# Squares of the gate norm summed in four groups of 32 tokens, one norm pass over 192 columns, and two state scalings placed earlier

## The chip, the cores and the metric

The kernel runs on one core of one Trainium2 chip. The metric is the device time of one execution in microseconds (us): the median of the runs of a kernel, lower is better. The core's engines are TensorE (PE in the profile, its weight loads PEld), VectorE (DVE), ScalarE (ACT), GpSimd (POOL) and SyncE (SP); each works through its own queue of instructions in order, and they wait for one another by semaphores.

## The reference

One layer of a streaming encoder is computed for 512 prompt frames and 64 frames of a running stream (576 tokens in all): a Mamba-2 state-space branch (SSD) and a latent-attention branch (MLA) side by side, an output projection, and a SwiGLU network. The change is about the norm behind the gate of the SSD branch, and about the scaling of the last SSD state:

```python
xbc, conv_new = causal_conv(xbc, conv_buf, p['conv_w'], p['conv_b'])
...
y, h_new = ssd_scan(xh, dt, A, Bm, Cm, ssm_h0)
y = y + d_skip[:, None] * xh
y = y.reshape(b, T, SSD_WIDTH) * jax.nn.silu(z)        # SSD_WIDTH = 512
y_ssd = rmsnorm(y, p['ssd_norm'])                       # per token, over 512 values
...
o_lat = mla_attend(q_lat, q_rope, q_pos, keys_c, keys_r, jnp.arange(P + T))
o = jnp.einsum('bthl,lhd->bthd', o_lat, p['w_uv']).reshape(b, T, MLA_WIDTH)
x = x + jnp.concatenate([y_ssd, o], axis=-1) @ p['w_out']
hf = rmsnorm(x, p['norm_ffn'])
x = x + (jax.nn.silu(hf @ p['w_gate']) * (hf @ p['w_up'])) @ p['w_down']

# ssd_scan, per chunk: w_end is exp(last - cum) * d
h_new = jnp.exp(last)[..., None, None] * h + jnp.einsum('blgh,blghp,blgn->bghpn', w_end, x, Bk)
```

All of it is float32.

## The kernel before

Features lie on partitions and tokens on columns: `xsd` holds the SSD branch's y as four tiles of 128 features x 576 tokens. The tokens come in five chunks: c = 0 to 3 are the prompt, 128 tokens each, and c = 4 is the stream, 64 tokens. Products that need more than one pass over the hi parts of the operands are written as hi x hi, hi x lo and lo x hi (`wh_`, `wl_` tiles, split on ACT by line 127 and on DVE by line 128). A matmul of plain float32 operands stands in the trace as two records.

The stages that the change touches follow one another. In the SSD stage (about 110 to 146 us) the last chunks' scores and states run on PE between the value products `ps_v` and the projections `ps_q`, `ps_k` of the first two attention head pairs. `gate(c)` (lines 624 to 635) multiplies y by the gate on DVE, squares it on ACT into `ysq`, sums the squares of the 512 features by four matmuls with a 128x128 matrix of ones (`ps_g`, line 634), which puts the sum of each token into all 128 partitions, and copies it on ACT into `ssy` (its rows in the trace name the tile R, since `ssy` is that buffer). `norm_y` (lines 806 to 811) turns `ssy` into the factor 1/sqrt(mean + eps), `Ry`, in two halves of 288 tokens. Each half is a chain through two engines: ACT lines 186, 188, 189, and DVE lines 187, 192, 193. `cat_tile(t)` scales a tile of y by `Ry` on DVE (line 814) and splits it in hi and lo parts (`cat_y`).

In the attention stage (146 to 222 us) PE makes scores `sc` of a head pair (line 719), ACT and DVE make the softmax `pr` of them (lines 702 to 709), PE transposes it (`ptp`, line 741), and the output projection `ps_o` (line 465) starts with the SSD half `cat_y`. The stream's scores are `sc_s`, its softmax `pr_4`, its transposes `ptp_s` (line 749). `qs` and `ks` are the copies of the projections `ps_q` and `ps_k` (lines 669, 673).

In the last stage (from 600 us) PE adds the last part of the down projection, `ps_l` (line 1143), DVE adds each finished bank to the stream x (line 1186) so that the bank is free for the next product, and the inputs of the last state products are scaled on DVE: `late_x` by line 500 (`to_chunk_end`) and line 503 (`decay`), called from `late_operands`; the products that read them run on PE after 625 us.

The order of the instructions on each engine is written out: the table ISSUE lists for PE, DVE, ACT, POOL and SP the numbers of the instructions in the order in which they are to be issued, and the table PLACES the buffer or PSUM bank that each tile takes. So the order is that of the tables, not that of the code.

Of the kernel before, what the change touches and what calls it, by code (L numbers as in the profile page):

```python
# [56 lines left out]
def hybrid_layer_kernel(ctx: ExitStack, tc: tile.TileContext, a, o):  # L57
# [206 lines left out]
    ssy = R1  # L264
# [1083 lines left out]
0651423651426340315406516235041350264531645302406124531260546312045123450612345014652051342603541350124365310462054260  # L1348
534132025104623562453163052412365401546210503421602541356041536510223405632140562056143241564032
# [15 lines left out]
0202102121201021020122100210121012012102101202012012012012012021021021021021021021021021021021021021021021021022101201  # L1365
202101
# [18 lines left out]
986 996-998 994-995 1042-1050 1031-1038 1023-1024 1055-1056 1051 1071-1088 1052-1054 1089-1100 1117-1119 1061-1063
1120 1057-1058 1067-1068 1059-1060 1126-1128 1064-1066 1121-1125 1069 1129-1152 1101-1104 1070 1225-1233 1115-1116
1234 1237 1235-1236 1238-1248 1153 1107-1110 1105-1106 1249-1260 1154 1172 1261-1272 1111-1114 1155-1157 1173-1175
1158-1171 1273-1281 1285-1286 1176-1179 1184-1185 1180-1183 1201-1202 1186-1188 1223 1189-1194 1287-1293 1195-1197
1224 1198-1200 1282-1284 1211-1216 1203-1210 1217 1314 1218-1220 1294 1221-1222 1295-1302 1315 1303 1316 1304-1313
1317-1318 1326-1328 1319 1338-1339 1344-1347 1340-1341 1348-1350 1342 1351 1343 1329 1320-1325 1330-1337 1352-1359  # L1390
1364 1360-1362 1365-1366 1363 1367-1389 1400 1390-1392 1401-1402 1393-1399 1403-1411 1424 1412-1423 1425-1429
1436-1437 1430-1431 1438 1432-1435 1568 1439-1443 1448 1444 1449-1452 1445 1453-1454 1446 1455-1456 1447 1457-1458
1583 1574 1580 1459 1577 1569 1460-1474 1575 1475-1482 1571 1484 1483 1485 1581 1486-1493 1496 1494 1497-1499 1495
1582 1584 1500-1502 1572 1570 1503 1576 1504-1505 1508 1573 1509 1506 1510-1511 1507 1512-1513 1601 1514-1518 1589
1519-1521 1578-1579 1522-1523 1602 1524-1527 1598 1532 1528 1533 1529 1534 1530 1599 1535 1603 1531 1585 1536-1537
1595 1538-1540 1590 1604 1541-1546 1596 1547-1548 1591 1610 1549-1551 1605 1556 1552-1553 1622 1557-1561 1611
1554-1555 1562-1564 1612 1565-1566 1600 1567 1592 1586 1593-1594 1597 1587 1606 1613 1616 1619 1617 1631 1623 1618
1588 1632 1625 1633 1624 1607 1637 1614 1626 1620 1627 1608-1609 1621 1654-1655 1638 1640 1646 1656 1643 1657-1658
1628-1629 1659 1647 1644 1660-1661 1615 1652 1634-1636 1662 1639 1663 1630 1664 1641 1665 1642 1645 1648-1650 1653
1690 1666-1668 1691-1693 1669 1678 1694 1651 1670 1695 1671 1696 1714 1679 1715 1672-1673 1697 1674 1680 1698 1675  # L1400
1681 1699 1676 1700 1682 1677 1716 1683 1717 1684 1718-1719 1685 1720 1686-1687 1702 1688-1689 1721 1703 1722 1701
# [274 lines left out]
```

## Time and profile before

| | before |
|---|---|
| time, median of 3 runs | 635.87 us (635.25 to 636.33) |
| profiled execution: its time / its span | 637.53 us / 635.6 us |
| TensorE granted clock over the span | 0.997 of full speed |
| PE busy | 624.6 us (98%) |
| PEld busy (beside PE) | 595.9 us (94%) |
| DVE busy | 551.9 us (87%) |
| ACT busy | 390.3 us (61%) |
| POOL busy | 70.5 us (11%) |

The span is the stretch from the first to the last instruction in the trace; 1.93 us (637.53 less 635.6) of the profiled execution's time lie around it. An engine's busy time is the sum over its instructions without overlaps, so that what is left of the span is its idle time. A row of the timeline gives the start of a run of like instructions, its length to the end of the last one, engine, line, what is written and read, the shape and the number; in square brackets stands how long the engine was idle before it and on whom it waited. Ends of matmuls are modelled, and a matmul's length holds its passage through the array, so the time that a run of matmuls costs is read from its start to the start of the next row.

### The profile page before, as it was taken

The page shows a single profiled execution, that of the slowest core. Times are in us where ns is not written, and L with a number is a line of the kernel's source. Part 1 is how long each engine was busy: PE and PEld are TensorE (multiplying, and loading weights), DVE is VectorE, ACT ScalarE, POOL GpSimd, SP SyncE. Part 2 cuts the span into 40 slices and gives each one's busy share as a digit, 9 for nine tenths or more (in the row PEclk, how much of TensorE's full clock was granted, in tenths as well). Part 3 has the DMA queues.
Part 4 walks back from the last instruction along what each step waited for, and adds up shares of the span by engine and source line. Part 5 has one row for each costly group of instructions (what it writes and reads, how often), then busy time and mean ns, then how long its engine had stood idle before and what let it go on. Part 6 is the DMA issues. An engine that isn't in the chain of part 4 may idle for free.

```text
span 635.6 us, 11925 instructions
## 1 busy us (share of the span) xinstructions
PE 624.6 (98%) x4613; PEld 595.9 (94%) x4613; DVE 551.9 (87%) x982; ACT 390.3 (61%) x751; POOL 70.5 (11%) x111
## 2 busy tenths in 40 slices
PE   9999999999999999999999999999999999999995
PEld 9899999885797899999999999999999999999994
DVE  6999995789767599999998997889888998999775
ACT  7655425789766479955656555656564666635464
POOL 1322122001010000000012002100111011100023
PEclk9999999999999999999999999999999999999998
DMA  9522175223220232232177436551756154734105
GB/s 317 201 51 79 35 209 163 99 72 130 104 80 35 66 125 76 88 112 68 34 197 166 120 100 150 141 139 52 188 138 157 68 165 117 168 100 160 45 1 182
DMA packets 32888, 74.63 MB, mean 117 GB/s; under 512 B 3882, under 2 KB 11960, under 8 KB 32576
## 3 DMA queue, kind: packets, MB, share of 16 engines
q1 hardware_dynamic: 26688, 62.73, 30.0%
q0 software_dynamic: 5424, 10.57, 9.3%
q8 instruction: 36, 0.59, 0.4%
q10 hardware_dynamic: 720, 0.57, 0.3%
q14 instruction: 20, 0.16, 0.1%
HBM read 59.14 MB, written 4.15 MB: 100 GB/s over the span
## 4 chain that ended last, share of the span: by engine, by line
PE 50%; DVE 1%; ACT 0%; DVEq 0%; issue 0%
PE ps_x L933 17%; PE ps_dx L1073 9%; PE ps_z L933 9%; PE ps_dz L1073 5%; PE ps_y L933 4%; PE ps_l L1143 4%; PE ps_dy L1073 2%; PE ps_s L507 0%; DVE x L1186 0%; PE ps_n L1249 0%; DVE x L1199 0%; DVE x L1203 0%; PE ps_n L1275 0%; DVE late_x L503 0%; DVE late_x L500 0%; PE ps_r L1317 0%
## 5 line engine op out<-in xcount | busy, mean ns | idle before, releaser
L933 PE MATMUL ps_x<-xop,wh_gu_S 128*128 128x288 f32 x504 | 126.3, 295 | 0.0
L933 PEld LDWEIGHTS ps_x<-xop,wh_gu_S 128*128 128x128 f32 x504 | 88.2, 188 | 0.7 <-ACT u L1002 0.2
L933 PE MATMUL ps_x<-xop,wl_gu_S 128*128 128x288 f32 x252 | 73.3, 295 | 0.0
L933 PE MATMUL ps_z<-xop,gu_a 128*128 128x288 f32 x252 | 61.7, 295 | 0.0
L127 ACT CAST wh_gu_S<-gu 128x1024 fp32r<-128x1024 f32 x44 | 46.2, 1053 | 14.8 <-PE ps_y L933 4.2
L128 DVE TENSOR_TENSOR wl_gu_S<-gu,wh_gu_S 128x1024 fp32r<-128x1024 f32 x44 | 52.9, 1219 | 0.8 <-ACT wh_gu_S L127 0.5
L933 PEld LDWEIGHTS ps_x<-xop,wl_gu_S 128*128 128x128 f32 x252 | 47.1, 188 | 0.0
L1086 POOL DMA_DIRECT2D x<-db x16 | 14.8, 927 | 279.6 <-ACT db L1079 249.5
L143 PE MATMUL ps_in<-xs,wh_in 128*128 128x288 f32 x256 | 45.5, 298 | 0.0
L933 PE MATMUL ps_y<-xop,wh_gu_A 128*128 128x288 f32 x168 | 44.9, 296 | 0.0
L933 PEld LDWEIGHTS ps_z<-xop,gu_a 128*128 128x128 f32 x252 | 43.5, 188 | 0.0
L933 PE MATMUL ps_z<-xop,wh_gu_S 128*128 128x288 f32 x168 | 43.4, 295 | 0.0
L933 PE MATMUL ps_x<-xop,wh_gu_A 128*128 128x288 f32 x168 | 42.7, 294 | 0.0
L127 ACT CAST wh_gu_A<-gu 128x1024 fp32r<-128x1024 f32 x22 | 23.1, 1051 | 24.6 <-PE ps_x L933 16.1
L143 PEld LDWEIGHTS ps_in<-xs,wh_in 128*128 128x128 f32 x256 | 37.7, 189 | 0.2
L933 PEld LDWEIGHTS ps_y<-xop,wh_gu_A 128*128 128x128 f32 x168 | 30.1, 188 | 0.1
L933 PEld LDWEIGHTS ps_z<-xop,wh_gu_S 128*128 128x128 f32 x168 | 29.7, 188 | 0.0
L128 DVE TENSOR_TENSOR wl_gu_A<-gu,wh_gu_A 128x1024 fp32r<-128x1024 f32 x22 | 26.8, 1219 | 3.3 <-ACT wh_gu_A L127 1.8
L465 PE MATMUL ps_o<-cat_y,wh_out 128*128 128x288 f32 x128 | 29.1, 313 | 0.5 <-DVE x L797 0.5
L933 PEld LDWEIGHTS ps_x<-xop,wh_gu_A 128*128 128x128 f32 x168 | 29.5, 188 | 0.0
L465 PE MATMUL ps_o<-cat_o,wh_out 128*128 128x288 f32 x128 | 27.5, 298 | 0.0
L143 PE MATMUL ps_in<-xs,wl_in 128*128 128x288 f32 x128 | 27.5, 296 | 0.0
(604 smaller groups left out, 1994.7 us busy)
## 6 DMA issues: line engine op xcount, KB each, us to landing
gu<-in_w_gu SPq DMA_DIRECT2D x44, 512.0 KB, 4.8
db<-in_w_down SPq DMA_DIRECT2D x16, 512.0 KB, 4.2
x<-db POOLq DMA_DIRECT2D x16, 288.0 KB, 6.4
x<-dc POOLq DMA_DIRECT2D x16, 288.0 KB, 4.3
wr_in<-in_w_in SPq DMA_DIRECT2D x8, 512.0 KB, 5.6
wr_out<-in_w_out SPq DMA_DIRECT2D x8, 512.0 KB, 3.2
cumb<-cumD SPq DMA_DIRECT2D x5, 512.0 KB, 4.8
x<-in_xT SPq DMA_DIRECT2D x2, 1152.0 KB, 6.5
```

What stands on the lines that cost most here:

```text
L127: act.copy(hi, raw)
L128: dve.tensor_tensor(lo, raw, hi.bitcast(F32), ALU.subtract)
L143: pe.matmul(ps[:m, hf, :n], w, x[:, hf * n : (hf + 1) * n], start=start and k == 0 and i == 0, stop=stop and k == last and i == 2,)
L465: pe.matmul(ps[:, :n], w, x[:, cols], start=not onto and k == 0 and i == 0, stop=onto or (k == len(terms) - 1 and i == 2), skip_group_chec ...
L933: pe.matmul(ps, p, q, start=not onto and first and kp == kps[0] and j == 0, stop=onto or (last and kp == kps[-1] and j == 2), skip_group_c ...
L1073: pe.matmul(ps, l, r, start=not onto and k == 0 and j == 0, stop=onto or (k == n - 1 and j == 2), skip_group_check=onto,)
L1086: pool.dma_start(x2[t], v, accum_op=ALU.add)
L1143: pe.matmul(ps, w, x[:, cols], start=first and not onto and k == 0 and i == 0, stop=onto or (last and k == len(terms) - 1 and i == 2), ski ...
```

## The change

Three things are changed.

First, in `gate` the squares of a prompt chunk (c < 4) are summed in four groups of 32 tokens: each of the four feature tiles takes four matmuls with 32 columns of ones as weights, and group j of the tokens lands on the PSUM partitions 32j to 32j+31 and on the same 32 columns. `ps_g` is 128x32 then, and chunk c's sums take 32 columns of `ssy`; the stream's 64 columns stand behind the prompt's 128. The stream's chunk (c = 4) is summed as before.

Second, `norm_y` makes the factor in one pass over these 192 columns, in place. The stream's 64 columns are copied on POOL; the prompt's factors, of which each group of 32 partitions holds other tokens, are spread over all partitions by four matmuls, whose weights are one column of the identity repeated 128 times (`ps_ry`), and copied on ACT into `Ry`.

Third, the tables: the two scalings of `late_x` for chunk 3 stand earlier on DVE, the split `wl_pair` of the third pair's weights too, and around the norm the rows are set anew. PE's and SP's order elsewhere is unchanged.

```diff
@@ gate(c) @@
         q = tmp(f"ysq{c}", 4 * L).rearrange("p (t l) -> p t l", t=4)
         act.activation(q, yv, AF.Square)
-        ps = bank("pp", f"ps_g{c}")[:, :L]
+        n = L // 4 if c < 4 else L
+        ps = bank("pp", f"ps_g{c}")[:, :n]
         for t in range(4):
-            pe.matmul(ps, ones, q[:, t], start=t == 0, stop=t == 3)
-        act.copy(ssy[:, tk], ps)
+            if c == 4:
+                pe.matmul(ps, ones, q[:, t], start=t == 0, stop=t == 3)
+                continue
+            for j in range(4):
+                pe.matmul(ps[32 * j : 32 * j + 32], ones[:, :32], q[:, t, j * n : j * n + n], start=t == 0, stop=t == 3)
+        act.copy(ssy[:, n * c : n * c + n] if c < 4 else ssy[:, P : P + n], ps)
@@ norm_y() @@
-        for hf in range(2):
-            cols = slice(hf * TH, (hf + 1) * TH)
-            norm_half(Ry[:, cols], ssy[:, cols], 512)
+        R = ssy[:, : P + TS]
+        norm_half(R, R, 512)
+        pool.tensor_copy(Ry[:, TP:], R[:, P:])
+        ps = bank("pp", "ps_ry")
+        for j in range(4):
+            pe.matmul(
+                ps.rearrange("p (c j n) -> p j c n", c=4, j=4)[:, j], ident[:, 32 * j : 32 * j + 1].to_broadcast([P, P]),
+                R[:, :P].rearrange("p (c n) -> p c n", c=4), start=True, stop=True,
+            )
+        act.copy(Ry[:, :TP], ps)
@@ ISSUE, PE (first changed line of many) @@
-793-816 765-768 817-824 857-859 831-834 860-862 825-830 863-864 835-837 865 878-881 838 866-868 839 843-850 869-871
+793-816 765-768 817-824 869-871 831-834 872-874 825-830 875-876 835-837 877 890-893 838 878-880 855-862 881-883
```

On PE, from the second score product of head pair 0 to the first transposes, these rows stood in this order before (`sc_3_1` is the second head's scores of the fourth query block, `ps_q_1` pair 1's second query projection):

```order
L719 MATMUL sc_3_1_1938<-ks_383,qs_382 128x512
L634 MATMUL ps_g_1873<-ysq_1871,ones 128x128
L719 MATMUL sc_1_0_1962<-ks_383,qs_382 128x256
L634 MATMUL ps_g_1882<-ysq_1880,ones 128x128 x4
L719 MATMUL sc_1_1_1964<-ks_383,qs_382 128x256
L719 MATMUL sc_2_0_1976<-ks_383,qs_382 128x384
L719 MATMUL sc_2_1_1978<-ks_383,qs_382 128x384
L634 MATMUL ps_g_1873<-ysq_1871,ones 128x128 x3
...
L465 MATMUL ps_q_1_1909<-cqn_487,wl_pair_1827 128x288
L725 MATMUL sc_s<-ks_383,qs_382 64x320 x2
L719 MATMUL sc_3_0_2014<-ks_385,qs_384 128x512
L741 MATMUL ptp_0_0_2033<-ident,pr_0_1996 128x128
```

And these stand there now:

```order
L724 MATMUL sc_3_1_1984<-ks_383,qs_382 128x512
L639 MATMUL ps_g_1897<-ysq_1895,ones 32x32 x16
L724 MATMUL sc_1_0_2008<-ks_383,qs_382 128x256
L639 MATMUL ps_g_1918<-ysq_1916,ones 32x32 x16
L724 MATMUL sc_1_1_2010<-ks_383,qs_382 128x256
L724 MATMUL sc_2_0_2022<-ks_383,qs_382 128x384
L724 MATMUL sc_2_1_2024<-ks_383,qs_382 128x384
...
L465 MATMUL ps_q_1_1957<-cqn_487,wl_pair_1851 128x288
L819 MATMUL ps_ry<-R_99,ident 128x4x32 x4
L730 MATMUL sc_s<-ks_383,qs_382 64x320 x2
L724 MATMUL sc_3_0_2060<-ks_385,qs_384 128x512
L746 MATMUL ptp_0_0_2079<-ident,pr_0_2042 128x128
```

The 32-token sums of a chunk stand in one block of 16 ahead of `sc_1_0` and of `sc_1_1`; nothing of them is left behind `sc_2_1`; the four `ps_ry` stand ahead of `sc_s`. The other two chunks' sums, of which before one matmul stood ahead of `ps_y` of chunk 1, two ahead of `ps_q_0`, two ahead of `ps_k_0` and three ahead of `ps_k_1`, are now one block of 16 ahead of `ps_k_0` and one ahead of `ps_k_1`.

On DVE, in the softmax of pair 0 with the norm chain (lines 187, 192 and 193) between its rows, these rows stood before, from the first norm half's last step on:

```order
L193 SCALAR_TENSOR_TENSOR Ry<-nr_u,nr_y 128x288
L187 TENSOR_SCALAR nr_v<-R_99 128x288
L709 TENSOR_SCALAR pr_2_1982<-pr_2_1982,sm 128x384
L702 TENSOR_REDUCE mx<-sc_s 128x1
L669 COPY qs_384<-ps_q_1_1909 64x288
L192 TENSOR_TENSOR nr_u<-nr_u,nr_v 128x288
L704 RECIPROCAL sm<-sm 128x2
L193 SCALAR_TENSOR_TENSOR Ry<-nr_u,nr_y 128x288
L709 TENSOR_SCALAR pr_0_1996<-pr_0_1996,sm 128x128
L702 TENSOR_REDUCE mx<-sc_3_0_2014 128x1
L704 RECIPROCAL sm<-sm 128x1
L814 SCALAR_TENSOR_TENSOR xsd<-xsd,par,Ry 128x576 x2
```

And these stand there now, from the one pass's last two steps on:

```order
L192 TENSOR_TENSOR nr_u<-nr_u,nr_v 128x192
L193 SCALAR_TENSOR_TENSOR R_99<-nr_u,nr_y 128x192
L707 TENSOR_REDUCE mx<-sc_0_1_2038 128x1
L709 RECIPROCAL sm<-sm 128x2
L714 TENSOR_SCALAR pr_2_2028<-pr_2_2028,sm 128x384
L674 COPY qs_384<-ps_q_1_1957 64x288
L709 RECIPROCAL sm<-sm 128x2
L714 TENSOR_SCALAR pr_0_2042<-pr_0_2042,sm 128x128
L707 TENSOR_REDUCE mx<-sc_s 128x1
L826 SCALAR_TENSOR_TENSOR xsd<-xsd,par,Ry 128x576 x2
L707 TENSOR_REDUCE mx<-sc_3_0_2060 128x1
```

The scaling of `pr_0`, for which PE's first transposes wait, no longer stands behind a second norm half and the reduction of `sc_s`.

On DVE near the end, with the sums of the down projection into x, these rows stood before (`ps_l_0` to `ps_l_3` belong to the first half of x, `ps_l_4` to the second):

```order
L500 TENSOR_TENSOR late_x_7349<-late_x_7349,hcw 64x512
L1186 TENSOR_TENSOR x_0_2045<-ps_l_0_7361,x_0_2045 128x320
L1186 TENSOR_TENSOR x_0_2045<-ps_l_1_7362,x_0_2045 128x320
L500 TENSOR_TENSOR late_x_7354<-late_x_7354,hcw 128x512
L503 TENSOR_TENSOR late_x_7354<-late_x_7354,hcw 128x512
L1186 TENSOR_TENSOR x_0_2045<-ps_l_2_7363,x_0_2045 128x320
L1186 TENSOR_TENSOR x_0_2045<-ps_l_3_7364,x_0_2045 128x320
L1186 TENSOR_TENSOR x_1_2047<-ps_l_4_7431,x_1_2047 128x320
```

And these stand there now:

```order
L500 TENSOR_TENSOR late_x_7395<-late_x_7395,hcw 64x512
L1198 TENSOR_TENSOR x_0_2091<-ps_l_0_7407,x_0_2091 128x320
L500 TENSOR_TENSOR late_x_7400<-late_x_7400,hcw 128x512
L503 TENSOR_TENSOR late_x_7400<-late_x_7400,hcw 128x512
L1198 TENSOR_TENSOR x_0_2091<-ps_l_3_7410,x_0_2091 128x320
L1198 TENSOR_TENSOR x_0_2091<-ps_l_1_7408,x_0_2091 128x320
L1198 TENSOR_TENSOR x_0_2091<-ps_l_2_7409,x_0_2091 128x320
L1198 TENSOR_TENSOR x_1_2093<-ps_l_4_7477,x_1_2093 128x320
```

The two scalings stand one sum earlier, and the sums of `ps_l_1` to `ps_l_3` are in another order.

## Rows read from the trace of the kernel before

**Rows 1.** The page's busy times: us, share of the span, number of instructions.

```profile
PE 624.6 (98%) x4613; PEld 595.9 (94%) x4613; DVE 551.9 (87%) x982; ACT 390.3 (61%) x751; POOL 70.5 (11%) x111
```

**Rows 2.** PE's waits: who for whom, us in total, times, longest.

```profile
PE ptp L741 <- DVE pr L709: 0.9, 1, 0.9
...
PE ps_l L1143 <- DVE x L1186: 0.2, 1, 0.2
PE ptp_s L749 <- DVE pr L709: 0.2, 1, 0.2
```

**Rows 3.** The tile ps_g: instructions, ns min/median/max, first and last start.

```profile
L634 PE MATMUL ps_g<-ysq,ones x40: 217/275/362, 122.6 to 149.9; 128*128 128x128 f32 x32, 128*128 128x64 f32 x8
```

**Rows 4.** Timeline of PE at the sums of squares and scores.

```profile
126.86 0.38 PE L634 MATMUL ps_g<-ysq,ones 128*128 128x128 f32 x2
127.17 1.09 PE L573 MATMUL ps_y<-E,xdt 128*64 128x128 f32 x16
128.20 0.45 PE L652 MATMUL ps_v<-wh_uv,ckv 128*64 128x512 f32 x1
...
146.71 1.05 PE L634 MATMUL ps_g<-ysq,ones 128*128 128x128 f32 x8
147.60 1.90 PE L719 MATMUL sc<-ks,qs 100*128 100x256 f32 x6
```

**Rows 5.** Timeline of PE at products with 64 columns of weights.

```profile
199.70 0.71 PE L777 MATMUL pvs<-pts,V 64*64 64x64 f32 x12
200.34 0.40 PE L465 MATMUL ps_o<-cat_y,wh_out 128*128 128x288 f32 x1
```

**Rows 6.** The same at 199.69 to 199.72 us: records under way.

```profile
199.70 0.27 PE L777 MATMUL pvs<-pts,V 64*64 64x64 f32 x2
```

**Rows 7.** Timeline of ACT and of DVE, first half of the norm.

```profile
148.42 0.53 ACT L186 ACTIVATE nr_y<-R,epsb 128x288 f32<-128x288 f32 x1
...
151.48 0.44 DVE L193 SCALAR_TENSOR_TENSOR Ry<-nr_u,nr_y 128x288 f32<-128x288 f32 x1
```

**Rows 8.** Timeline of DVE, second half of the norm and the scaling behind it.

```profile
153.78 0.46 DVE L193 SCALAR_TENSOR_TENSOR Ry<-nr_u,nr_y 128x288 f32<-128x288 f32 x1
154.16 0.28 DVE L709 TENSOR_SCALAR pr<-pr,sm 128x128 f32<-128x128 f32 x1
```

**Rows 9.** Timeline of PE from sc_s to the first output products.

```profile
151.57 0.76 PE L725 MATMUL sc_s<-ks,qs 100*64 100x320 f32 x4
152.45 1.13 PE L719 MATMUL sc<-ks,qs 100*128 100x512 f32 x2
154.50 0.66 PE L741 MATMUL ptp<-ident,pr 128*128 128x128 f32 x4 [0.92 <-DVE pr L709]
...
157.63 0.41 PE L749 MATMUL ptp_s<-ident,pr 128*64 128x128 f32 x2 [0.22 <-DVE pr L709]
```

**Rows 10.** Timeline of DVE around the split wl_pair.

```profile
141.91 0.46 DVE L669 COPY qs<-ps_q 64x288 f32<-64x288 f32 x1 [0.41 <-ACT qs L669]
...
147.76 0.55 DVE L128 TENSOR_TENSOR wl_pair<-wr_pair,wh_pair 128x384 fp32r<-128x384 f32 x1
```

**Rows 11.** Timeline of DVE in the last stage.

```profile
608.74 0.49 DVE L1186 TENSOR_TENSOR x<-ps_l,x 128x320 f32<-128x320 f32 x1 [1.83 <-PE ps_l L1143]
609.14 0.68 DVE L500 TENSOR_TENSOR late_x<-late_x,hcw 128x512 f32<-128x512 f32 x1
609.74 0.69 DVE L503 TENSOR_TENSOR late_x<-late_x,hcw 128x512 f32<-128x512 f32 x1
610.34 1.68 DVE L1186 TENSOR_TENSOR x<-ps_l,x 128x320 f32<-128x320 f32 x4
```

**Rows 12.** Timeline of PE in the last stage.

```profile
610.71 0.60 PE L1143 MATMUL ps_l<-pr,wh_dl 128*128 128x320 f32 x3
611.15 0.31 PE L1143 MATMUL ps_l<-pr,wl_dl 128*128 128x320 f32 x1
611.68 0.39 PE L1143 MATMUL ps_l<-pr,wh_dl 128*128 128x256 f32 x1 [0.22 <-DVE x L1186]
```

More of the change, by code (lines that the diff above doesn't have):

```diff
@@ L1385 @@
[L1385 to L1389, printed above, removed]
@@ new lines @@
+863-866 884-889 926-928 867-868 894-897 929-931 839-854 932-934 914-925 898-913 935-937 947-956 938-943 957 944-946
+958-960 993-1001 1012-1013 961-976 1014 977-992 1015-1019 1002-1011 1020-1022 1024-1027 1023 1035-1036 1028 1032-1033
+1051 1039-1041 1029-1031 1034 1063 1052-1054 1037 1042-1043 1064-1069 1044 1055-1062 1070-1074 1077-1082 1045
+1091-1093 1038 1048-1050 1046-1047 1094-1102 1083-1090 1075-1076 1107-1108 1103 1123-1140 1104-1106 1141-1152
+1169-1171 1113-1115 1172 1109-1110 1119-1120 1111-1112 1178-1180 1116-1118 1173-1177 1121 1181-1204 1153-1156 1122
@@ new lines @@
+1277-1285 1167-1168 1286 1289 1287-1288 1290-1300 1205 1159-1162 1157-1158 1301-1312 1206 1224 1313-1324 1163-1166
+1207-1209 1225-1227 1210-1223 1325-1333 1337-1338 1228-1231 1236-1237 1232-1235 1253-1254 1238-1240 1275 1241-1246
+1339-1345 1247-1249 1276 1250-1252 1334-1336 1263-1268 1255-1262 1269 1366 1270-1272 1346 1273-1274 1347-1354 1367
+1355 1368 1356-1365 1369-1370 1378-1380 1371 1390-1391 1396-1399 1392-1393 1400-1402 1394 1403 1395 1381 1372-1377
+1382-1389 1404-1411 1416 1412-1414 1417-1418 1415 1419-1441 1452 1442-1444 1453-1454 1445-1451 1455-1463 1476
@@ new lines @@
+1464-1475 1477-1481 1488-1489 1482-1483 1490 1484-1487 1620 1491-1495 1500 1496 1501-1504 1497 1505-1506 1498
+1507-1508 1499 1509-1510 1635 1626 1632 1511 1629 1621 1512-1526 1627 1527-1534 1623 1536 1535 1537 1633 1538-1545
+1548 1546 1549-1551 1547 1634 1636 1552-1554 1624 1622 1555 1628 1556-1557 1560 1625 1561 1558 1562-1563 1559
+1564-1565 1653 1566-1570 1641 1571-1573 1630-1631 1574-1575 1654 1576-1579 1650 1584 1580 1585 1581 1586 1582 1651
+1587 1655 1583 1637 1588-1589 1647 1590-1592 1642 1656 1593-1598 1648 1599-1600 1643 1662 1601-1603 1657 1608
@@ new lines @@
+1604-1605 1674 1609-1613 1663 1606-1607 1614-1616 1664 1617-1618 1652 1619 1644 1638 1645-1646 1649 1639 1658 1665
+1668 1671 1669 1683 1675 1670 1640 1684 1677 1685 1676 1659 1689 1666 1678 1672 1679 1660-1661 1673 1706-1707 1690
+1692 1698 1708 1695 1709-1710 1680-1681 1711 1699 1696 1712-1713 1667 1704 1686-1688 1714 1691 1715 1682 1716 1693
+1717 1694 1697 1700-1702 1705 1742 1718-1720 1743-1745 1721 1730 1746 1703 1722 1747 1723 1748 1766 1731 1767
+1724-1725 1749 1726 1732 1750 1727 1733 1751 1728 1752 1734 1729 1768 1735 1769 1736 1770-1771 1737 1772 1738-1739
@@ new lines @@
+2908-2909 2919 2890-2892 2910 2896-2898 2911 2879-2880 2899 2893 2900 2912-2913 2901-2902 2914 2881 2903 2915
+2904-2905 2920 2916 2921-2923 2917 2942-2943 2924 2930-2935 2944-2945 2936 2954 2925 2955 2926 2946-2947 2937 2948
+2927 2938 2928-2929 2956 2949-2951 2939 2952 2940 2953 2957 2941 2958-2963 2978 2964-2969 2990 2970-2971 2979
+2972-2975 2980 2976-2977 2981 3002 2982 2991 2983 3003 2992 3004 2984 2993-2995 2985 2996 3005 2997 2986 2998 3006
+3080 2999-3001 3007 3081 3008 2987 3082 2988 3009 3026-3028 2989 3029 3010-3011 3083 3030 3012 3031-3032 3084
@@ L1505 @@
+4342 4325 4343 4326 4344 4327 4371 4359 4328-4329 4348-4349 4345 4330-4331 4358 4350 4383-4384 4351 4372 4352-4353
+4332 4354 4360 4333 4355 4361 4373-4374 4385 4356 4375-4376 4395 4357 4386 4396 4387-4388 4362-4363 4389 4364 4397
+4365-4366 4377-4378 4367 4379 4398 4368 4399 4380 4369 4390 4400 4391 4401 4370 4392 4381 4393 4382 4394 4402 4407
+4403-4406 4408-4430
 """,
@@ new lines @@
+829 843 852 842 836-837 844 840 838 854 839 831 830 841 845 847 855 832 856 874 849 859 851 848 850 857-858 861 864
+878 870 860 865 871 875 867 873 866 876 869 872 883 879 884 890 882 900 868 877 881 896 902 880 903 891-892 897 904
+893 885 894 912 899 908 901 905 886 907 906 862 898 913-914 916 863 915 910 887 911 917-918 909 888 921 895 920 930
+919 922 889 931 925 924 932 923 926-927 933 928-929 934 937 935-936 940 938-939 942-943 941 945 944 947 946 948-949
+951 956 952 950 954-955 953 958 960-961 964-965 957 959 962 966 963 967-978
@@ L1565 @@
+684 686 688 690 681 687 685 693 695-697 691 683 698-699 679 700 707 689 694 701 703 705-706 702 708-712 692 704
+713-714 717 716 715
 """,
     "POOL": """
[L1567 to L1568 removed]
+0-3 7 18 28 4 8 5 9 6 10 26-27 11 29 12-17 20-22 19 23-25 31 30 32-42 53 55 57 59 54 56 58 60 43-52 61-74 76 75 77-78
+80 79 81-86 88 87 89-90 92 91 93-94 96 95 97-107 109-110 108 112 111
```

312 lines of the change are left out of this document (140 added, 172 removed).

## The prediction

> **What bounds the kernel now.** I read the busy times first: PE is busy for 624.6 us of the 635.6 us span, 98%, while DVE has 87% and ACT 61% [rows 1]. So PE's instruction stream is the time, and an edit counts by what it takes out of that stream or by what it makes the stream wait. The list of PE's waits comes next. It is short: the first transposes `ptp` wait 0.9 us for DVE's scaling of a softmax, the stream's `ptp_s` 0.2 us for the like, and one down product `ps_l` 0.2 us for DVE's sum into x [rows 2]. All three lie where the change acts. Then the timeline of PE at those places, to see what a matmul costs from its start to the start of the next row, and DVE's and ACT's beside it, to see who is late.
>
> **What is removed on PE.** `ps_g` has 40 records, 32 of them for the prompt (128x128) and 8 for the stream, which stay [rows 3]. Eight of them run from 146.71 us to the start of the next product at 147.60: 0.89 us, 111 ns each [rows 4]. 32 x 0.111 = 3.55 us go.
>
> **What is added on PE: four blocks of 16 small matmuls.** A matmul has two records, so a block has 32, 128 in all. No row of before has a product with 32 columns of weights and 32 of tokens. The nearest are those with 64 columns of weights, of which two run side by side. `ps_y` does 16 records of 128 columns in 1.03 us (127.17 to 128.20) [rows 4]; one after another at 111 ns they would take 1.78 us, in pairs 0.89 us, so they run in pairs and 0.14 us goes for entering and leaving. The two records ahead of it take 0.31 us (126.86 to 127.17) in place of 0.22, so 0.09 us more goes for the change from full weights to half ones. `pvs`, 12 records of 64 columns, takes 0.64 us (199.70 to 200.34) [rows 5]: six pairs at half of 111 ns are 0.33 us, and 0.31 us is for its two shapes. Two records are under way within 0.03 us of its start [rows 6]. If four groups run side by side as two do, and the time of a pass goes with its columns (111 ns x 32/128 = 28 ns), a block of 32 records is 8 rounds x 28 ns = 0.22 us, plus 0.14 + 0.09 us for the two changes, plus, as an estimate, 0.10 us for the full weights loaded behind it with nothing to cover them: 0.55 us. Four blocks cost 2.2 us. The lower bound is rounds alone, 0.9 us. The upper is each record at what one of `pvs` costs with everything in it, 0.64/12 = 53 ns: 128 x 0.053 = 6.8 us. I take 2.2, since the rows with tiles side by side are the nearest and both fit the pair count. The sums of squares thus save 3.55 - 2.2 = 1.3 us of PE.
>
> On the changes of shape the Trainium skill says the same, that changing the tiling mode drains the engine (TensorEngine Tiling (Array Packing), Key Properties); by the same page's section on instruction overhead one should not take a tiling factor from a dimension that is already small, because a matmul of one column costs as much as one of 60. This speaks against 32 columns: as an estimate from that page the 32 x 4 records would be no cheaper than with 60 columns, about 0.2 us more for each block than my 0.55, and the sum would be 0.8 us worse (52 ns a round in place of 28).
>
> **The four `ps_ry`.** Eight records of full weights and 128 columns at 111 ns: 0.9 us added, in PE's queue ahead of `sc_s` and all that follows. They also add a wait: they read the finished factor R. Before, L186 of the first half began at 148.42, 0.82 us after the end of the second squares block (147.60) [rows 4, 7], and the half was done at 151.48 + 0.44 = 151.92: 3.5 us from end to end, mostly softmax rows between its links. The new pass has the same links and neighbours; 192 columns in place of 288 spare some 0.1 us in each of five (a DVE row of 128 columns takes 0.28 us, one of 288 takes 0.46 [rows 8]), so 3.0 to 3.5 us. At the end of the second squares block PE is ahead by 0.65 us (2.9 us of the old records are out by there, 2.2 us in), at 146.95. R is then ready at 146.95 + 0.82 + 3.0 to 3.5 = 150.8 to 151.3. PE would reach `ps_ry` at 151.57 - 1.3 = 150.27 [rows 9]. It waits 0.5 to 1.0 us; I take 0.8. What the blocks cost doesn't change this wait, since R and PE's way to `ps_ry` both start from their end. So `sc_s` starts at about 151.57 - 1.3 + 0.8 + 0.9 = 151.97, 0.4 us late. Queued behind are `sc_s`, pair 1's first score product, and the transposes.
>
> **What this gives back at the transposes.** Before, PE stood at 153.58 with nothing to do until 154.50, because `pr_0` was scaled only at 154.16 to 154.44, right behind the second half of the norm, whose last link ended at 154.24 [rows 8, 9]. That half is gone, and the scaling stands five short rows behind the new last link: 151.3 + 1.5 + 0.28 = 153.1. PE comes at 153.58 + 0.4 = 153.98 and does not wait. The 0.92 us fall out: -0.5 us net. The 0.22 us of `ptp_s` wait for a scaling that stands behind the same rows; DVE has lost a norm half of three rows there, so I count that wait as gone too: -0.7 us. `Ry` comes later than the factor by a copy on ACT and one on POOL; `cat_y` waits for it, but DVE's scaling of y started at about 155 before, behind `pr_0`, and has a microsecond.
>
> The split `wl_pair`, 0.55 us, moves on DVE to a place where DVE stood idle for 0.41 us waiting for ACT [rows 10]. It covers that gap and delays the gate products by some 0.1 us; PE has a long score product ahead of the squares there, so this costs nothing. Without that cover it would be 0.55 us.
>
> **The last stage.** DVE stood idle for 1.83 us ahead of the sum at 608.74, then did the two scalings (0.68 and 0.69 us) and then four sums in a row to 612.0 [rows 11]. PE wants a bank that the third of these sums frees: its row at 611.68 starts 0.53 us after the one before, where the pace is 0.147 us (610.71 to 611.15 for three) [rows 12]. 0.38 us is lost. With the scalings in the idle gap the sums start as soon as PE ends a bank, and the wait goes: -0.4 us. If the scalings' data came too late for that, the gain would be nothing.
>
> **Sum.** -1.3 + 0.8 + 0.9 - 0.92 - 0.22 - 0.38 = -1.1 us. PE ahead by a microsecond will catch up with DVE and ACT somewhere in the attention stage; I give back 0.1. The profiled execution's 637.53 us would become 636.5. It is 1.66 us above the median of the runs shown, so the median 635.87 becomes 634.9 us. What a measurement can tell from no change is 0.2%, 1.3 us: I expect no measurable change, on the fast side.
>
> **Rivals.**
> 1. *R is ready in time.* If ACT and DVE do the norm links faster, or the blocks cost nearer their lower bound, the 0.8 us wait for `ps_ry` falls away: -1.9 us, 634.0. For it: DVE loses half of the norm. Against it: the links alternate between two engines with softmax rows between. Chance 0.16.
> 2. *Records start one by one.* If a record cannot start before some time after the last, side by side or not, the blocks cost more. At 35 ns a record, two thirds of the `pvs` price, they take 4.5 us in place of 2.2. Result: -1.1 + 2.3 = +1.2 us, 637.1. The two records under way within 0.03 us speak against it for two groups; for four no row speaks. Chance 0.15. The Trainium skill has a floor of this kind, 25 ns from start to start however small the matmul (TensorE: Matmul & The Clock Gate, on seeing the gap between matmuls); no row here shows it at 25 ns, and the two starts lie about that near to each other, which decides nothing.
> 3. *The small matmuls do not overlap* (the other side). At the upper bound of 53 ns a record the blocks cost 6.8 us: -1.1 + 4.6 = +3.5 us, 639.4. It decides from -1.1 + (x - 2.2) = 0 on, x = 3.3 us, 26 ns a record. Chance 0.08.
> 4. *The gain is given back*: PE ahead meets an attention stage in which DVE and ACT set the pace, and only part of the last stage's 0.4 us stays: -0.2 us, 635.7. Against it: PE has no wait above 0.9 us in all of that stage. Chance 0.12.
>
> **How the numbers follow.** The forecast (-0.5 to -1.5 us) has 0.49. Faster by over 0.2% needs -1.3: a third of the forecast's chance and nearly all of rival 1, 0.31. Slower by over 0.2% is rival 3 and nearly half of rival 2: 0.14. The rest, 0.55, is no change. The range from 633.8 (rival 1 and a little) to 637.0 (up to rival 2, of which half lies above) leaves out rival 3, that half and the tails. The forecast alone is 634.4 to 635.4.
>
> **What would show it.** In the changed profile: the four blocks of `ps_g` at about 0.55 us from start to next row (step of the sums right), against 1.1 (rival 2) or 1.7 (rival 3). A wait of PE before `ps_ry` for DVE of 0.5 to 1.0 us, and none at `ptp` and `ptp_s`. No wait at the first `ps_l` of 256 columns in the last stage, and DVE's two scalings before 608.5. New waits of PE between 158 and 222 us would mean rival 4. The forecast is wrong if the blocks cost over a microsecond each, or if `ps_ry` waits over two, for instance for a copy on ACT that stands behind softmax rows.

## The result, and the profile after

The changed kernel is slower: 638.25 us median of 8 runs (637.84 to 639.09) against 636.47 us of 8 runs of the kernel before (the 635.87 us of the section on time is the median of the first three of them), ratio 1.0031 with a 95% interval of 1.0020 to 1.0042, which is 1.3 to 2.7 us more. The forecast was 634.9 us, with 633.8 to 637.0 as the range. The profiled execution took 638.88 us, with a span of 637.1 us at a mean clock of 0.995 (0.997 before).

The page's busy times, and a line from the list of whom PE waits for (us in total, times, longest):

```profile
PE 625.4 (98%) x4717; PEld 595.3 (93%) x4717; DVE 551.0 (86%) x979; ACT 389.3 (61%) x749; POOL 71.1 (11%) x112
```

```profile
PE sc L724 <- ACT pr L708: 2.0, 2, 1.7
```

The waits at `ptp`, `ptp_s` and `ps_l` [rows 2] are gone, as forecast. In their place stands one that the forecast did not have: PE waits 1.7 us for ACT at a score product. The timeline of PE of the changed kernel shows where:

```profile
146.68 0.46 PE L639 MATMUL ps_g<-ysq,ones 128*32 128x32 f32 x32
147.07 2.91 PE L724 MATMUL sc<-ks,qs 100*128 100x256 f32 x8
150.30 0.49 PE L724 MATMUL sc<-ks,qs 100*128 100x128 f32 x2 [0.32 <-ACT pr L708]
...
151.76 1.13 PE L819 MATMUL ps_ry<-R,ident 128*128 128x128 f32 x8 [0.17 <-DVE R L193]
152.81 0.76 PE L730 MATMUL sc_s<-ks,qs 100*64 100x320 f32 x4
...
154.47 0.60 PE L746 MATMUL ptp<-ident,pr 128*128 128x128 f32 x4
154.91 1.67 PE L724 MATMUL sc<-ks,qs 100*128 100x512 f32 x4
158.30 0.91 PE L724 MATMUL sc<-ks,qs 100*128 100x384 f32 x2 [1.73 <-ACT pr L708]
...
162.46 0.75 PE L724 MATMUL sc<-ks,qs 100*128 100x256 f32 x2
```

The rows of the kernel before to set beside them (the last six records of sums, the last score of pair 0, and two scores of pair 1):

```profile
149.33 0.83 PE L634 MATMUL ps_g<-ysq,ones 128*128 128x128 f32 x6
...
150.35 0.49 PE L719 MATMUL sc<-ks,qs 100*128 100x128 f32 x2
...
156.49 0.81 PE L719 MATMUL sc<-ks,qs 100*128 100x384 f32 x2
...
159.32 0.60 PE L719 MATMUL sc<-ks,qs 100*128 100x256 f32 x2
```

A block of small sums takes 0.39 us from its start to the next row. The transposes start at 154.47 where they started at 154.50 [rows 9], without a wait. Then PE makes `sc_3_1` and `sc_2_0` of pair 1 and stands still: the bank that `sc_2_1` is to take still holds `sc_3_0`. ACT and DVE of the same stretch:

```profile
155.35 0.67 ACT L157 ACTIVATE cat_y<-xsd 128x576 fp32r<-128x576 f32 x1
155.92 0.57 ACT L748 COPY pt<-ptp 128x512 f32<-128x512 f32 x1
156.39 0.62 ACT L712 ACTIVATE pr<-pr,sm 128x384 f32<-128x384 f32 x1
156.91 0.67 ACT L157 ACTIVATE cat_y<-xsd 128x576 fp32r<-128x576 f32 x1
157.48 0.68 ACT L708 ACTIVATE pr<-sc,mx 128x512 f32<-128x512 f32 x1
```

```profile
154.05 1.54 DVE L826 SCALAR_TENSOR_TENSOR xsd<-xsd,par,Ry 128x576 f32<-128x576 f32 x2
155.51 0.68 DVE L707 TENSOR_REDUCE mx<-sc 128x1 f32<-128x512 f32 x1
```

The last row of ACT is the exponential that empties the bank of `sc_3_0`. Its maximum stands on DVE behind two scalings of y, and itself on ACT behind two casts of `cat_y`, a copy and a scaling. None of these rows waits: each engine goes from one to the next, so that it is their length that delays the exponential, 2.1 us of rows on ACT (155.35 to 157.48). Before, in the timeline of ACT of the kernel before, it came 2 us sooner, right behind the scaling of `pr_3`:

```profile
154.80 0.71 ACT L707 ACTIVATE pr<-pr,sm 128x512 f32<-128x512 f32 x1
155.41 0.67 ACT L703 ACTIVATE pr<-sc,mx 128x512 f32<-128x512 f32 x1
```

The windows of PE over the changed kernel (stretch, its length, PE's busy us and instructions, granted clock as a share of full speed, DMA share, GB/s) show a second loss behind the first:

```profile
157.00:158.30 1.30, 0.00 (x0) 1.00 0.00 0
158.30:159.30 1.00, 1.00 (x4) 0.94 0.06 16
159.30:162.40 3.10, 3.10 (x15) 0.50 0.00 0
```

After PE's idle stretch of 1.73 us (to 158.30) and one more us at work, the granted clock is 0.50 for 3.1 us, the lower of its two levels (1.2 in place of 2.4 GHz). Row against row of before, PE is level at the transposes (-0.03 us), 1.81 us late at the row that waited (158.30 against 156.49), and 3.1 us late at 162.46 (159.32 before). So 1.8 us are there with the wait, and 1.3 us more come in the stretch at the lower clock. The clock is not the price of all of these 1.3 us: in experiment 3, which keeps the clock up with the bank as late, a wait of 0.84 us for the next bank takes the place of a part of them.

By the end the delay falls from 3.1 to 1.5 us in the two profiles. That is partly the last stage (0.5 us; the first `ps_l` of 256 columns now starts 0.15 us after the row ahead of it, where before it was 0.53 [rows 12]):

```profile
613.18 0.31 PE L1155 MATMUL ps_l<-pr,wl_dl 128*128 128x320 f32 x1
613.33 0.28 PE L1155 MATMUL ps_l<-pr,wh_dl 128*128 128x256 f32 x1
```

and partly 0.9 us between 225 and 350 us, in rows that the change does not touch. Experiment 4, whose kernel differs from that of before only after 600 us, has the same 0.9 us against that one profile: they belong to the profiled execution of before, not to the change.

### The profile page after: what moved, and what is told of

Same layout as the page of the kernel before. It is cut to its first block, busy times and chain, and to the rows that moved or that the text cites. A ratio compares the mean times of both kernels' runs of the same rounds, so it can differ in the third digit from the quotient of the medians.

```text
span 637.1 us, 12132 instructions
## 1 busy us (share of the span) xinstructions
PE 625.4 (98%) x4717; PEld 595.3 (93%) x4717; DVE 551.0 (86%) x979; ACT 389.3 (61%) x749; POOL 71.1 (11%) x112
## 4 chain that ended last, share of the span: by engine, by line
PE 92%; ACT 3%; DVE 3%; issue 1%; DMA 1%; POOL 0%; DVEq 0%; POOLq 0%; ACTq 0%
PE ps_x L945 21%; PE ps_z L945 10%; PE ps_dx L1085 9%; PE ps_in L143 8%; PE ps_o L465 7%; PE ps_y L945 5%; PE ps_dz L1085 5%; PE ps_l L1155 4%; PE ps_z L465 3%; PE ps_first L143 3%; PE ps_dy L1085 2%; PE sc L724 2%; PE ps_p L945 2%; PE pv L771 1%; PE ptp L746 1%
```

## The experiments

All comparisons are with the kernel before on the same chip, as a ratio with a 95% interval; the changed kernel stands at 1.0031.

**1. Only the order of four softmax rows.** The theory after the result: ACT's and DVE's new order keeps a score bank from PE, and the idle stretch brings the low clock; the sums and the norm are not to blame. The rival: the spread by `ps_ry` makes `sc_s` and all behind it late, so that no order helps.

```diff
 ACT  pr_3 scaled (pair 0)
+ACT  exponential of sc_3_0 (pair 1)
 ACT  cat_y0, pt_0, pr_2, cat_y1
-ACT  exponential of sc_3_0 (pair 1)
+ACT  exponential of sc_3_1 (pair 1)
 ACT  pt_2, cat_y2
-ACT  exponential of sc_3_1 (pair 1)
 DVE  first scaling of y
+DVE  maximum of sc_3_0
 DVE  second scaling of y
-DVE  maximum of sc_3_0
 DVE  reciprocal
+DVE  maximum of sc_3_1
 DVE  pr_4 scaled, cat_y0, third scaling of y
-DVE  maximum of sc_3_1
```

> The changed kernel with four rows moved and nothing else: on ACT the two exponentials of pair 1's first score banks (sc_3_0, sc_3_1) stand ahead of the first cast of cat_y and ahead of the copy of pt_2, as before the change, and on DVE their two maxima stand between and behind the first two scalings of y. Theory (the order on ACT and DVE keeps a score bank from PE): PE's wait of 1.73 us at 156.6 us for the exponential that frees the bank goes, no half clock follows, and the stretch to 163 us is 3 us shorter: some 635.5 us, 0.4 to 1.2 us below the kernel before. Rival (the spread by row matmuls makes sc_s and all behind it late, whatever the order): a wait of over 1 us stays at the same place and the time stays above the kernel before.

Measured: 635.34 us, ratio 0.9979 (0.9970 to 0.9988). The wait is gone; PE's timeline and its window over the slow stretch:

```profile
154.28 0.60 PE L746 MATMUL ptp<-ident,pr 128*128 128x128 f32 x4
154.72 2.40 PE L724 MATMUL sc<-ks,qs 100*128 100x512 f32 x6
...
159.01 0.70 PE L724 MATMUL sc<-ks,qs 100*128 100x256 f32 x2
```

```profile
159.30:162.40 3.10, 3.10 (x24) 1.00 0.00 0
```

The six score records run through and the clock stays at its upper level. By the two ratios the same arithmetic with these rows moved is 3.3 us faster than the changed kernel (0.0052 of 637 us), and 0.8 to 1.9 us faster than before, a little more than expected. The traces agree: from the first transposes to the row of 162.46 us in the changed kernel PE took 7.99 us there and takes 4.73 us here, 3.3 us less. `ps_ry` is still ahead of `sc_s`: the rival falls.

**2. Only ACT's exponential, by two rows.** A shorter wait in place of none.

```diff
 ACT  cat_y0, pt_0
+ACT  exponential of sc_3_0 (pair 1)
 ACT  pr_2 scaled, cat_y1
-ACT  exponential of sc_3_0 (pair 1)
```

> The changed kernel with one row moved: ACT's exponential of sc_3_0 of pair 1 stands ahead of the scaling of pr_2, two rows sooner; DVE's maximum stays behind two scalings of y. Theory: the bank is free some 1 us sooner (ACT at about 156.4 in place of 157.5), PE's wait falls from 1.7 to about 0.6 us. If the half clock behind it comes from the length of the wait, it goes too and the kernel is 2.5 us faster than the changed one; if it comes from something else there, the kernel gains only the 1.1 us of the wait.

Measured: 637.01 us, ratio 1.0000 (0.9991 to 1.0009), some 2 us below the changed kernel. The timeline of PE:

```profile
156.94 0.91 PE L724 MATMUL sc<-ks,qs 100*128 100x384 f32 x2 [0.66 <-ACT pr L708]
...
160.47 0.70 PE L724 MATMUL sc<-ks,qs 100*128 100x256 f32 x2 [0.86 <-ACT pr L708]
```

The wait fell by 1.07 us as expected and the clock stayed at 1.00 from 154 to 164 us. But a second wait appeared for the next bank (`sc_1_0` for the exponential of `sc_3_1`), which the changed kernel, slower by the clock, reached only when it was free (no wait at 162.46 us). It took a part of the expected 2.5 us.

**3. Work in the wait.** PE multiplies idly while it would wait; everything else is the changed kernel.

```diff
         act.copy(Ry[:, :TP], ps)
+        for _ in range(8):
+            pe.matmul(ps[:, :P], ident, ones, start=True, stop=True)
 PE   sc_3_1, sc_2_0 (pair 1)
+PE   the eight idle matmuls
 PE   sc_2_1 (pair 1)
```

> The changed kernel with 8 idle matmuls more (identity times ones, 16 records of 128 columns, read by nothing) in PE's queue right ahead of the row that waits 1.73 us, so that PE computes through the wait. Theory (the half clock from 159.3 to 162.5 us is the price of the idle stretch before it): the wait for the bank stays, 158.3 us as before, but the clock stays at full level, and the kernel is about 1.5 us faster than the changed one though it does more. Rival (the clock falls for another reason, such as the small matmuls at 146 us or the transposes): the half clock stays and the time does too.

In the profile the low clock is gone. PE's timeline and a window:

```profile
155.68 1.95 PE L825 MATMUL ps_ry<-ones,ident 128*128 128x128 f32 x16
157.57 0.91 PE L724 MATMUL sc<-ks,qs 100*128 100x384 f32 x2
...
161.10 0.70 PE L724 MATMUL sc<-ks,qs 100*128 100x256 f32 x2 [0.84 <-ACT pr L708]
```

```profile
159.30:162.40 3.10, 2.25 (x17) 1.00 0.00 0
```

Full clock where the changed kernel had 0.50, with the bank still late. From the first transposes (153.74 us here) to the row of 161.10 PE takes 7.36 us, against 7.99 us in the changed kernel: the clock alone gives back 0.6 us, not 1.5, since PE now waits for the next bank. That profiled execution took 637.58 us. The median of its 9 runs was 639.85 us (637.58 to 642.21), ratio 1.0046 (1.0029 to 1.0064): not faster than the changed kernel, against the theory; the two intervals overlap. A second look:

> The changed kernel with idle matmuls in the wait once more, for a second profile, since its executions took 637.6 to 642.2 us and the first profile was the fastest of them. Theory (PE's idle stretch brings the half clock): the clock is full from 156 to 164 us again, and a slower execution loses its time elsewhere. Rival (the fill does not keep the clock): the half clock stands at 159 us as in the changed kernel.

It took 637.17 us (on another chip, where the kernel before has a median of 637.08), again with a clock of 1.00 in each microsecond from 154 to 168 us. Both profiles bear out that the clock stays up where PE has work. That this makes the kernel faster is not shown: what the longer executions lose, and where, no profile caught, and stays open.

**4. Only the last stage.** The kernel before with DVE's five rows in the new order.

```diff
 DVE  late_x (chunk 4), sum of ps_l_0
-DVE  sum of ps_l_1
 DVE  late_x scalings of chunk 3 (L500, L503)
-DVE  sum of ps_l_2
 DVE  sum of ps_l_3
+DVE  sum of ps_l_1
+DVE  sum of ps_l_2
 DVE  sum of ps_l_4
```

> The kernel before with the change's last part alone: DVE's two scalings of late_x for chunk 3 and the sum of ps_l_3 stand ahead of the sum of ps_l_1. Theory: PE's wait at the first 256-column ps_l (0.38 us lost to its pace, and the weights' load behind it) goes: -0.3 to -0.5 us. Rival: the time is handed back in the final norm, whose rows follow 13 us later: 0.

Measured: 635.85 us, ratio 0.9988 (0.9979 to 0.9998), 0.1 to 1.3 us faster. The timeline of PE there, without a wait:

```profile
609.77 0.31 PE L1143 MATMUL ps_l<-pr,wl_dl 128*128 128x320 f32 x1
609.91 0.28 PE L1143 MATMUL ps_l<-pr,wh_dl 128*128 128x256 f32 x1
```

Row against row of before, PE gains 0.5 us across these rows (from 1.39 to 1.87 us ahead), and keeps it to the end. The rival falls.

**5. Full sums in place of small ones.** The kernel of experiment 1 with `ones` of 128 columns again, four matmuls to a block.

```diff
...
-            for j in range(4):
-                pe.matmul(ps[32 * j : 32 * j + 32], ones[:, :32], q[:, t, j * n : j * n + n], start=t == 0, stop=t == 3)
+            pe.matmul(ps, ones, q[:, t], start=t == 0, stop=t == 3)
...
```

> The kernel of the first experiment (softmax rows sooner) with each chunk's squares summed again by four matmuls of full weights over 128 columns, at the same four places; only 32 of the 128 columns are copied on, so the factors of the norm are not those of the reference, which changes no instruction behind. Theory of the forecast (a block of 16 small matmuls costs 0.55 us with its two changes of shape, one of four full matmuls 0.89): each block 0.34 us dearer, and what the score banks cover of it at 147 to 150 us does not show: 0.4 to 1.4 us slower than the first experiment. Rival (the small ones are paced by their records): the full sums are the faster ones.

Measured: 636.95 us, ratio 1.0009 (0.9998 to 1.0019), against 0.9979 for experiment 1: by the two ratios 1.9 us slower, more than the 0.4 to 1.4 expected. The last block of each, between the score rows ahead of it and behind it, in experiment 1:

```profile
145.87 0.70 PE L724 MATMUL sc<-ks,qs 100*128 100x256 f32 x2
146.50 0.46 PE L639 MATMUL ps_g<-ysq,ones 128*32 128x32 f32 x32
146.89 2.91 PE L724 MATMUL sc<-ks,qs 100*128 100x256 f32 x8
```

and with full sums:

```profile
147.12 0.60 PE L721 MATMUL sc<-ks,qs 100*128 100x256 f32 x2
147.56 1.05 PE L635 MATMUL ps_g<-ysq,ones 128*128 128x128 f32 x8
148.45 2.57 PE L721 MATMUL sc<-ks,qs 100*128 100x256 f32 x8
```

From score to score that is 1.02 us against 1.33. Row against row of experiment 1, the four blocks add 0.46, 0.30, 0.45 and 0.31 us, 1.5 us in all, and PE is still 1.4 us later at the last score: the score banks covered none of it. The forecast had 0.34 each. So 16 small matmuls with their changes of shape cost about 0.5 us where four full ones cost 0.89. By the Trainium skill (TensorEngine Tiling (Array Packing), on instruction overhead) one should not take a tiling factor from a dimension that is already small. Here the split of 128 tokens into four times 32 paid, by 0.4 us a block. The 0.75 us a block that the prediction's estimate from that page comes to (0.55 and 0.2 more) is not borne out.

**6. The spread behind `sc_s`.**

```diff
-PE   ps_ry (4)
 PE   sc_s
+PE   ps_ry (4)
 PE   sc_3_0 (pair 1)
-ACT  copy of Ry
 ACT  pr_1, pr_0 scaled
+ACT  copy of Ry
```

> The kernel of the first experiment with the four row matmuls ps_ry behind sc_s on PE in place of ahead of it, and their copy on ACT behind two scalings of the softmax. Theory (PE waits at ps_ry for the factor, 0.16 us shown and 0.3 us against its pace): that wait goes and sc_s starts 1.2 us sooner; the transposes come 0.3 us sooner, and DVE's first scaling of y 0.7 us later: -0.3 to 0 us against the first experiment. Rival (the spread sets the start of the output products through cat_y): a new wait at the first ps_o, 0.5 us slower.

Measured: 635.83 us, ratio 0.9993 (0.9984 to 1.0002), not below experiment 1. `ps_ry` does not wait any more (a row of 8 records at 153.02 without a wait), but PE now waits at a score bank, and ACT, whose exponential frees it, waits for DVE:

```profile
157.38 0.91 PE L724 MATMUL sc<-ks,qs 100*128 100x384 f32 x2 [0.39 <-ACT pr L708]
```

```profile
156.55 0.69 ACT L708 ACTIVATE pr<-sc,mx 128x512 f32<-128x512 f32 x1 [0.43 <-DVE mx L707]
```

On DVE the maximum of `sc_3_0` stands behind the first scaling of y, which waits 0.23 us for the later copy of `Ry` (at 155.04 us). So here, and not in the changed kernel, the spread itself delays a score bank. What the rival blames is at work, but at another place than it says: the first `ps_o` (158.42 us) does not wait.

**7. A projection where PE waits for banks.**

```diff
 PE   sc_1_1
+PE   ps_q_1 of pair 1 (6)
 PE   sc_2_0, sc_2_1, sc_0_0, sc_0_1
-PE   ps_q_1 of pair 1 (6)
 PE   sc_s, ps_ry (as in experiment 6)
```

> The sixth experiment's kernel with pair 1's projection ps_q_1 (six matmuls, 1 us) moved on PE from behind the last scores of pair 0 to between sc_1_1 and sc_2_0. Theory (with the sums of squares gone from between the scores, PE waits there for ACT's exponentials to free a bank, about 1 us that the list of waits shows only in part): the projection fills that time, the last score still comes at about 150.3 us, and the transposes 0.5 us sooner: 0.4 to 0.8 us below the first experiment. Rival (PE's products are all that counts there): no change.

Measured: 635.75 us, ratio 0.9987 (0.9978 to 0.9996): no better than experiment 1. PE's timeline:

```profile
145.67 0.70 PE L724 MATMUL sc<-ks,qs 100*128 100x256 f32 x2
...
150.19 0.49 PE L724 MATMUL sc<-ks,qs 100*128 100x128 f32 x2 [0.49 <-ACT pr L708]
...
153.39 0.60 PE L746 MATMUL ptp<-ident,pr 128*128 128x128 f32 x4
...
156.35 0.91 PE L724 MATMUL sc<-ks,qs 100*128 100x384 f32 x2 [0.86 <-ACT pr L708]
```

The first half of the theory holds for the most part. From the score row ahead of the last block of sums to the last score of pair 0 it is 4.52 us (145.67 to 150.19) against 4.25 in experiment 1 (145.87 to 150.12), although a microsecond of projection was put between: 0.7 us of it found room in waits for ACT's exponentials. The transposes come 0.7 us sooner, counted from the same score row (7.72 us, against 8.41 in experiment 1 and 8.03 in experiment 6). But then PE waits 0.86 us for the next exponential: ACT and DVE set the pace of the stretch as a whole, and what PE gains ahead it waits behind.

**8. A longer wait in the kernel before.** It says whether an idle stretch alone brings the low clock, in a kernel without small matmuls.

```diff
             norm_half(Ry[:, cols], ssy[:, cols], 512)
+        dve.tensor_tensor(Ry, Ry, Ry, ALU.max)      # on DVE ahead of the scaling of pr_0
```

> The kernel before with one needless row on DVE ahead of the scaling of pr_0 (the factor's maximum with itself, 576 columns, some 0.75 us), so that PE's wait at the first transposes grows from 0.92 to about 1.7 us. Theory (PE's clock halves after an idle stretch of that length): a half clock of some 3 us follows, and the kernel is about 0.75 + 1.5 = 2.2 us slower than before. Rival (the half clock of the changed kernel came from its small matmuls): the clock stays full and the kernel is 0.75 us slower at the most.

Measured: 638.45 us (636.72 to 641.42 in 10 runs), ratio 1.0035 (1.0019 to 1.0050), 1.2 to 3.2 us slower. The first profile has the wait of 1.72 us at the transposes and no low clock. A second look:

> The kernel before with one needless row on DVE once more, for a second profile. Its wait of 1.7 us at the transposes had a full clock behind it in the first profile, in an execution of 637.6 us with a mean clock of 0.997, while other executions took up to 641.4 us at 0.992. Theory (the wait is followed by a half clock in some executions): a profile of a slower execution shows half clock from some 1 us behind the wait on; one of about 637 us shows none. Rival: the slower ones lose it elsewhere.

The wait and the window behind it, of the first look:

```profile
155.26 0.66 PE L741 MATMUL ptp<-ident,pr 128*128 128x128 f32 x4 [1.72 <-DVE pr L709]
```

```profile
156.00:160.00 4.00, 3.79 (x21) 1.00 0.02 6
```

and of the second:

```profile
154.96 0.66 PE L741 MATMUL ptp<-ident,pr 128*128 128x128 f32 x4 [1.72 <-DVE pr L709]
```

```profile
156.00:160.00 4.00, 4.00 (x13) 0.57 0.01 2
```

The same kernel, the same wait of 1.72 us, and the low clock behind it in one profile and not in the other. The second was taken on another chip, but the runs on the first chip spread in the same way, as their mean clocks show below. So an idle stretch of PE does bring the lower clock without any small matmul, but not each time. In these two profiles it cost little: the one with the low clock took 637.69 us, the other 637.60. It was 1.3 us later by 160 us, and the rows from 192 to 230 us took most of that up. The spread of the ten runs goes with their mean clock: 636.72 and 636.90 us at 0.998, 640.31 and 641.42 us at 0.992. Which stretch the longest ones lost, no profile shows.

**9. The gate norm alone.** Experiment 1 with the last stage in the order of before.

```diff
 DVE  late_x (chunk 4), sum of ps_l_0
+DVE  sum of ps_l_1
 DVE  late_x scalings of chunk 3
+DVE  sum of ps_l_2
 DVE  sum of ps_l_3
-DVE  sum of ps_l_1
-DVE  sum of ps_l_2
```

> The kernel of the first experiment (softmax rows sooner) with the last stage's five DVE rows back in the order of before: what is left of the change is the gate norm, with the rows of the softmax in their old places. Theory (the last stage is worth 0.4 to 0.8 us, the gate norm itself some 0.5 us): 0.3 to 0.8 us below the kernel before, 0.5 us above the first experiment, with PE's wait of 0.2 us at the first 256-column ps_l back. Rival (the whole gain of the first experiment is the last stage's): the time of the kernel before.

Measured: 636.15 us, ratio 0.9984 (0.9973 to 0.9996): 0.3 to 1.7 us faster than before, with the `ps_l` wait of 0.2 us back in the list. The gate norm, with the softmax rows in their old places, is a gain by itself, if a small one; the rival falls, though 1.0 is near the interval's end. With the last stage (experiment 1) the middle value is 0.0005 lower, which these intervals do not tell apart.

**10. The changed kernel a second time.**

> The changed kernel once more, for a second profile of it. Theory (the order of ACT keeps the bank, in every execution): the wait of 1.7 us stands at the same row. Whether the half clock follows it is what this looks at: if the length of the wait alone decides, it follows again, 3 us long; if it comes by the wait's place against something else, it may be missing or of another length.

It took 640.3 us, on the chip on which the kernel before has a median of 637.08. The wait of 1.73 us stands at the same row (158.70 us), and the low clock follows it again: the granted clock is 0.56 from 159 to 160 us, 0.50 to 162 and 0.74 to 163.

```profile
160.00:161.00 1.00, 1.00 (x6) 0.50 0.00 0
```

## Why the prediction was wrong

**The step that failed** is the part on what the change gives back at the transposes, and with it the sum, which carries PE from `ptp` to the end with -0.7 us. It followed DVE's order as far as the scaling of y and looked at PE's next two listed waits. It never followed the two new orders into pair 1's softmax. There the rows that free PE's score banks had been put behind the norm's consumers: on ACT the exponential of `sc_3_0` behind two casts of `cat_y`, on DVE its maximum behind two scalings of y. The prediction checked only whether these consumers have their `Ry` in time, and they have: the first scaling of y starts at 154.05 us, 1.1 us sooner than before, and no row of the two engines waits there for `Ry`. What it did not ask is who stands behind them now. The order lists of DVE in the section on the change show it for the maximum. In place of the sum's -0.7 us from `ptp` on came a wait of 1.73 us, and PE was 3.1 us late at 162.46 us. Experiment 1 settles this: four rows moved, nothing else, and the sign turns from +2.0 to -1.3 us. That this is near the forecast of -1.0 us does not bear the sum out: at 159 us, where the sum has PE 0.7 us ahead, experiment 1 has 0.3 us (159.01 against 159.32), of which 0.17 us were there at 120 us, ahead of all changed rows.

**The clock** was in no term and no rival. The wait of 1.7 us was followed by some 3 us at the lower level in both profiles of the changed kernel. Experiments 1 to 3 each took the idle stretch away or shortened it, and each profile had the upper level. Experiment 8 shows that a stretch of the same length brings it in a kernel without small matmuls, in one profile of two. That the wait is the cause is thus shown; what decides whether the clock falls after a wait of 1.7 us is not. Its share of the 3.1 us at the row of 162.46 us is the smaller one: 0.6 us by experiment 3, and 1.1 us between the second profiles of the two kernels (8.45 against 7.36 us from the first transposes to that row). The mean clocks of the runs agree, as an estimate. In the profiles a low stretch takes 0.0027 off the mean, and the low clock behind the last product, which all of them have, 0.0022 or more. Four of the eight runs of the changed kernel have 0.996 or 0.998, too much for both; they took 637.84 to 638.25 us, still over 1.3 us above the median of before, and the four with 0.994 or 0.995 took 637.98 to 639.09.

**The four blocks** were sized rightly: 0.55 us forecast, about 0.5 us by experiment 5 (0.39 us to the next row, and the rest at their ends). Of the 0.55 us, no row shows the 0.10 us for the weights loaded behind a block; only the block as a whole was measured. Rivals 2 and 3, the small matmuls paced one by one, were wrong: 32 records in 0.39 us are 12 ns each, below the 25 ns that rival 2 quotes and its own 35 ns.

**What the sums save** did not reach `ps_ry`, a second step that failed. The forecast had PE there 1.3 us sooner; it came to the last score of pair 0 at 150.30 against 150.35 before. Behind the second block PE was still 0.53 us ahead (147.07 against 147.60 [rows 4]), about the forecast's 0.65. From there to the last score it took 3.23 us, and before, with six records of sums between the scores (149.33 to 150.00), only 2.75. PE is held there by the exponentials that free the banks, though the list shows only 0.32 us of it as a wait. Before, the sums filled that time, so removing them saved what PE had to spare. Experiment 7 shows the same from the other side: 0.7 us of a projection fits in. Ahead of these scores it is otherwise: there experiment 5's dearer blocks cost their full 1.5 us.

**`ps_ry`**: the wait was put at 0.5 to 1.0 us. 0.17 us is listed, because PE itself came late; the eight records and the wait together made `sc_s` 1.24 us late, where 0.4 us was forecast from a start 1.3 us ahead, a cost of 1.3 in place of 1.7 us. The factor was ready at about 151.6 us (forecast 150.8 to 151.3).

**The transposes** did not wait, as forecast, and started 0.03 us sooner in place of 0.5 us. `ptp_s` did not wait either. The split `wl_pair` cost nothing, as forecast: no wait of PE is listed between 120.11 and 150.30 us.

**The last stage** was right: the wait went; 0.5 us in the trace against 0.4 forecast. DVE's two scalings start at 608.86 and 609.46 us, not before 608.5 as the sign had it, but PE is 2 us later there than before.

**Rival 4** named the right place in the test that it gave, new waits of PE between 158 and 222 us, but as a gain given back, not as a loss of three microseconds, and with no row behind it.

## What to carry to other kernels

Where an order of instructions is set anew, follow each PSUM bank round: who fills it, who empties it, and what now stands ahead of the one that empties it on its engine. A chain made shorter can still be put in front of work that another engine waits for. Before counting a matmul's removal as a gain, ask whether the matmul filled a wait for a bank; and look at the granted clock behind a long wait of TensorE, since it can be lower for some microseconds there.

## What the runs showed of the hardware

Matmuls with 32 columns of weights, on four groups of PSUM partitions, run side by side: 32 records of 32 columns take 0.39 us, 12 ns a record, while a record of full weights over 128 columns takes 111 ns, of which 32 columns are a share of 28 ns (an estimate). A wait of PE of 1.72 us was followed by a granted clock of 0.50 in three profiles of four (two of the changed kernel, one of two of experiment 8); waits of 0.66 to 0.92 us (the kernel before and experiments 2, 3 and 7) were not followed by it in any profile taken. In the changed kernel's first profile it stood at 0.50 for 3.1 us, from about 1 us behind the wait, while PE was busy throughout.
